# Retention fed in steps between MLA's blocks of queries; block 2's output projection in one pass

## The chip, the cores and the metric

The kernel runs on one core of one Trainium2 chip. The metric is the time of one execution on the device, in microseconds (us), as the median of several executions. The core has a matrix engine (PE, with its weight loads on a track of their own, PEld), a vector engine (DVE), a scalar engine (ACT), GpSimd (POOL), and SyncE (SP), which here only starts DMA transfers. Each engine carries out its own queue in order. PE's clock is granted at one of two levels, 1.2 and 2.4 GHz; the profile shows it as a share of full speed.

## What is computed

Two transformer blocks of two layers each over 512 tokens of 1024 features. The change lies in the second block. One of its layers, from the reference:

```python
hn = rms_norm_2(h, attn_norm[l])
proj = hn @ w_in[l]
p_a, p_b, p_c = ...                        # columns for RWKV-7, retention, MLA
y_a, v_first = rwkv7_mixer(p_a, ...)       # 256 features
y_b = retention_mixer(p_b, positions)      # 256 features, 4 heads, chunks of 128 tokens
y_c = mla_mixer(p_c, positions, ...)       # 512 features, 8 heads, causal softmax
mix = jnp.concatenate([y_a, y_b, y_c], axis=-1)
h = h + mix @ w_out[l]
hn = rms_norm_2(h, ffn_norm[l])
gu = hn @ w_gate_up[l]
h = h + (jax.nn.silu(gu[..., :D_FF_2]) * gu[..., D_FF_2:]) @ w_down[l]
```

Retention, per head and chunk: scores within the chunk times a decay mask times the values; the sum of the chunks before, decayed, as a 64x64 state that the decayed queries read; then a norm per head and a gate.

## The kernel before

Activations lie with features on the partitions: a tensor of 1024 features is eight tiles ("k-tiles") of 128 x 512. Every float32 product is made of three matmuls, high part by high part, low by high and high by low: `split` (L154, L155) makes the parts of an activation, `load_w` (L133 to L140) loads a weight tile by SP, casts it on ACT (`whi`) and subtracts on DVE (`wlo`). There are three buffers for each of `whi` and `wlo`, two for the raw weights, five for `tm`.

The program is written as a sequence, but a scheduler orders the instructions of each engine before the run: an instruction may go ahead of others that were written before it when its inputs are there. A pool of tiles that is opened where another was closed uses the same memory.

A layer of block 2 runs in these steps. RWKV is woven with the input projections of MLA and then of retention (`weave`, `ret_inputs`). `mla` (L1733) then goes over 8 heads, each in four blocks of 128 queries: scores (tags `l` and `m`, four matmuls), softmax on DVE and ACT, transposes (`t`), values (`o`); after each score block `feed` (L177) takes `rate` steps of the filler, which is the rest of `ret_inputs`, one step for two k-tiles of a projection. Two heads share the tile `yt`, which is one buffer (`y=(0,)`): `normalised` turns the softmax sums, sends them by DMA to memory and back as a broadcast, multiplies on POOL and writes the pair to `mixd` by DMA; the next pair's output is written into the same tile. After MLA, `retention` (L1682) runs for its two pairs of heads with banks `l`, `m`, `t`, `o`. Then eight tiles of the residual `X` are loaded again (L1890), in layer 0 also scaled (L1896, eight DVE instructions); the six tiles of RWKV and MLA are read back from `mixd` into `tm` (L1900) and split. `residual` makes the eight outputs from six k-tiles (weights `w2out`, adds at L869); a second pass over the eight outputs adds retention's two k-tiles (weights `w2outb`, adds at L1914) and calls `prepare` for each output: a square on ACT (L1097), its sum on POOL (L1098), and the split `hh`, `hl` for the feed-forward network (L1105, L1106), whose first matmuls read `hh` and `hl` of all eight outputs.

## Time and profile before

| | |
|---|---|
| median of 3 runs | 3397.08 us (3393.93 to 3398.56) |
| the profiled execution | 3398.97 us, of which its span is 3397.2 us |
| busy share of the span | PE 97%, PEld 81%, DVE 57%, ACT 36%, POOL 12% |
| mean granted clock of PE | 0.985 |
| layer 0 of block 2: MLA, retention, output projection | about 2148 to 2299 us of the span |
| layer 1 of block 2: the same | about 2871 to 3026 us |

A row of a timeline gives the start, the duration, the engine, the line, the operation, output and inputs, the shapes and the count, and in brackets the idle time of the engine just before and what ended it. A row of the stages gives the busy time of each engine in one stretch, with the number of instructions, the granted clock (1.00 is 2.4 GHz), the busy share of the DMA engines and their GB/s. Idle time of PE in a stretch is its length less PE's busy time.

### The profile page before, as it was taken

To read this page: it belongs to the slowest core of one execution; us is meant where nothing else is said; L and a number is where in the kernel's file an instruction comes from. 1 tells how busy PE (TensorE), PEld (TensorE's weight loads), DVE (VectorE), ACT (ScalarE), POOL (GpSimd) and SP (SyncE) were. 2 spreads that over 40 slices of the span, in tenths; PEclk is the share of its full clock that TensorE was granted. 3 is DMA by queue.
4 is the path that set the end of the run, shared out by engine and by line. 5 is a ranking of instruction groups with operands and counts; after the bars stand their busy time and mean duration, and the time that the engine had idled before them with its cause. 6 is when DMAs were issued, how large, how long until landed. Compare 5 with 4: busy or idle time off the path is not lost. (4 is left out here: it accounts for less than half of the span.)

```text
span 3397.2 us, 48949 instructions
## 1 busy us (share of the span) xinstructions
PE 3311.8 (97%) x19412; PEld 2747.3 (81%) x19412; DVE 1930.5 (57%) x3356; ACT 1233.3 (36%) x2196; POOL 398.5 (12%) x362
## 2 busy tenths in 40 slices
PE   7999999999999999999999999999999999999998
PEld 4888888888888888889888877777888777778887
DVE  6667765756444567757333466764434566754344
ACT  3566632311212346634222332532222332632222
POOL 4231000100000101101000301111101111121001
PEclk9999999999999999999999999999999998999999
DMA  6434373334334243253232323323233323422322
GB/s 215 132 114 125 109 264 109 112 118 132 123 128 129 73 137 106 91 187 111 93 90 98 125 80 98 118 89 93 89 98 99 109 69 97 128 89 94 94 98 81
DMA packets 138110, 385.86 MB, mean 114 GB/s; under 512 B 17492, under 2 KB 29268, under 8 KB 137880
## 3 DMA queue, kind: packets, MB, share of 16 engines
q1 hardware_dynamic: 134552, 372.15, 34.7%
q0 software_dynamic: 3328, 10.57, 1.0%
q8 instruction: 153, 2.51, 0.3%
q14 instruction: 77, 0.63, 0.1%
HBM read 331.56 MB, written 43.76 MB: 110 GB/s over the span
## 5 line engine op out<-in xcount | busy, mean ns | idle before, releaser
L139 ACT CAST whi<-raw 128x1024 fp32r<-128x1024 f32 (+4 forms) x436 | 435.4, 999 | 1288.5 <-PE b L158 870.7
L140 DVE TENSOR_TENSOR wlo<-raw,whi 128x1024 fp32r<-128x1024 f32 (+4 forms) x431 | 510.4, 1184 | 382.2 <-ACT whi L139 355.2
L158 PE MATMUL b<-hl,whi 128*128 128x512 f32 (+1 forms) x1760 | 688.2, 391 | 6.0 <-DVE hl L1106 5.5
L158 PE MATMUL b<-hh,whi 128*128 128x512 f32 (+1 forms) x1760 | 692.5, 393 | 0.0
L158 PE MATMUL b<-hh,wlo 128*128 128x512 f32 (+1 forms) x1760 | 686.9, 390 | 0.0
L158 PEld LDWEIGHTS b<-hl,whi 128*128 128x128 f32 x1760 | 333.6, 190 | 81.4 <-DVE hl L1106 8.3
L158 PEld LDWEIGHTS b<-hh,whi 128*128 128x128 f32 x1760 | 333.9, 190 | 78.4 <-issue 4.8
L158 PEld LDWEIGHTS b<-hh,wlo 128*128 128x128 f32 x1760 | 333.4, 189 | 75.5 <-issue 0.7
L158 PE MATMUL b<-ah,whi 128*128 128x512 f32 (+1 forms) x864 | 317.8, 368 | 0.0
L158 PE MATMUL b<-ah,wlo 128*128 128x512 f32 (+1 forms) x864 | 317.7, 368 | 0.0
L158 PE MATMUL b<-al,whi 128*128 128x512 f32 (+1 forms) x864 | 317.6, 368 | 0.0
L158 PEld LDWEIGHTS b<-ah,whi 128*128 128x128 f32 x864 | 162.3, 188 | 29.9
L158 PEld LDWEIGHTS b<-al,whi 128*128 128x128 f32 x864 | 162.3, 188 | 29.9
L158 PEld LDWEIGHTS b<-ah,wlo 128*128 128x128 f32 x864 | 162.3, 188 | 29.8
L947 DVE TENSOR_TENSOR tm<-tm,b 128x512 f32<-128x512 f32 (+1 forms) x112 | 70.0, 625 | 202.3 <-PE b L158 195.9
L408 DVE SCALAR_TENSOR_TENSOR wlo<-raw,silb 128x1024 f32<-128x1024 f32 x128 | 157.3, 1229 | 41.4 <-DMA raw<-in_ada1b 22.2
L158 PE MATMUL l<-hh,whi 128*128 128x512 f32 (+1 forms) x472 | 176.4, 374 | 0.8 <-DVE stB L697 0.3
L158 PE MATMUL l<-hl,whi 128*128 128x512 f32 (+1 forms) x472 | 173.2, 367 | 0.0
L158 PE MATMUL l<-hh,wlo 128*128 128x512 f32 (+1 forms) x472 | 172.7, 366 | 0.0
L508 DVE TENSOR_TENSOR pt<-t,pt 128x384 fp32r<-128x384 f32 (+2 forms) x272 | 131.1, 511 | 35.9 <-ACT pt L507 34.1
L158 PE MATMUL b<-hc,whi 128*128 128x256 f32 x800 | 141.5, 279 | 0.0
L467 DVE TENSOR_REDUCE st<-S 128x1 f32<-128x768 f32 (+2 forms) x160 | 121.7, 763 | 34.8 <-PE S L158 34.1
(572 smaller groups left out, 5784.0 us busy)
## 6 DMA issues: line engine op xcount, KB each, us to landing
raw<-in_wgu SPq DMA_DIRECT2D x92, 512.0 KB, 3.3
raw<-in_w2gu SPq DMA_DIRECT2D x88, 512.0 KB, 3.4
raw<-in_ada1b SPq DMA_DIRECT2D x48, 512.0 KB, 3.2
raw<-in_w2in SPq DMA_DIRECT2D x38, 512.0 KB, 3.5
raw<-in_ada0b SPq DMA_DIRECT2D x32, 512.0 KB, 4.2
raw<-in_wg SPq DMA_DIRECT2D x32, 512.0 KB, 3.9
raw<-in_w2d SPq DMA_DIRECT2D x32, 512.0 KB, 3.5
raw<-in_wd SPq DMA_DIRECT2D x24, 512.0 KB, 3.5
```

Source lines behind the costliest of these rows:

```text
L139: self.nc.scalar.copy(hi, raw)
L140: getattr(self.nc, self.lo).tensor_tensor(lo, raw, hi.bitcast(F32), op=ALU.subtract)
L158: self.nc.tensor.matmul(out, l, r, start=start, stop=stop)
L408: nc.vector.scalar_tensor_tensor(junk, raw, 0.5, self.silb[:, v], op0=ALU.mult, op1=ALU.mult, accum_out=m[:, w, k, v:v + 1])
L467: nc.vector.tensor_reduce(nm, S[:, lo:hi], axis=AX.X, op=ALU.max, negate=True)
L508: nc.vector.tensor_tensor(o, src, h.bitcast(F32), op=ALU.subtract)
L947: nc.vector.tensor_tensor(b, th, pu, op=ALU.mult)
```

## The change

Retention becomes a part of the filler. `retained` runs `ret_inputs` and then `retention`, which gives way at six places for each pair of heads, takes its banks from tag `b` (two banks), and writes its two k-tiles as number 2 and 3 into tiles that are set aside before MLA. `counted` counts the steps taken before MLA, and the rate in MLA is (52 less these) / 30 instead of 1. After MLA a pool of eight banks `b` is opened; the six other k-tiles are loaded and split, now ahead of the scaling of `X`. The output projection has one pass: the weights of the eight outputs are of eight k-tiles each and come in through `next_w`; outputs 0, 1 and 2 are opened with k-tiles 0 to 6, then each gets k-tile 7 (MLA's last pair of heads), then outputs 3 to 7 follow with eight k-tiles. `prepare` follows each output. The second pass and its weights are gone. The number of matmuls of the projection is the same (8 x 8 x 3 for a layer).

```diff
--- before.py
+++ after.py
@@ -33,6 +33,7 @@
+RSTEPS = 52
@@ -1239,10 +1240,17 @@
-    @staticmethod
-    def kept(gen, results):
-
-        results.append((yield from gen))
+    def counted(self, gen):
+
+        self.taken = 0
+        for x in gen:
+            self.taken += 1
+            yield x
+
+    def retained(self, l, pool, es, H, bc, rs, tab, mix):
+
+        src = yield from self.ret_inputs(l, [pool, pool], H, bc, rs, tab)
+        yield from self.retention(l, self.rets, src, mix)
@@ -1677,13 +1685,12 @@
-                + [d[f"w2v{l}"][c] for c in range(2)] + [w[11], w[12]])
+                + [d[f"w2v{l}"][c] for c in range(2)] + [w[11], w[12]] + [d[f"w2out{l}"][n] for n in range(KD)])
     def retention(self, l, pool, src, mix):
...
-            qd = self.t(pool, [128, 3, 128], F32, "rq", 2)
+            qd = self.t(pool, [128, 3, 128], F32, "rq", 1)
...
-            ps = self.bank("t")
+            ps = self.bank("b")
...
-            kt = self.t(pool, [128, 3, 128], F32, "rkt", 2)
+            kt = self.t(pool, [128, 3, 128], F32, "rkt", 1)
...
-            inner = [self.bank(next(tags)) for _ in range(2)]
+            yield
+            inner = [self.bank("b") for _ in range(2)]
...
+            yield
+            st = self.bank("b")[:, :192].rearrange("p (c e) -> p c e", e=64)
...
+            yield
+            pso = self.bank("b")
...
+            yield
+            bc = (yield from self.head_rstd_steps([sq], 1.0 / 64, EPS, "b", tok=(rt, rt2)))[0]
...
-            self.split(y, mix[0]["lat"][6 + p], mix[1]["lat"][6 + p])
+            self.split(y, mix[0]["lat"][2 + p], mix[1]["lat"][2 + p])
+            yield
@@ -1859,60 +1871,69 @@
-                    self.filler = self.streamed("L", self.kept(self.ret_inputs(l, [retp, retp], H, bc, rs, tab_r), results))
+                    self.filler = self.counted(self.streamed("L", self.retained(l, retp, es_rets, H, bc, rs, tab_r, mix)))
...
+            mp = self.pool(es_mix, "mixr")
+            for i in (2, 3):
+                mix[0]["lat"][i], mix[1]["lat"][i] = mixed(mp)
+            self.rets = self.pool(es_rets, "rets", "right")
             with ExitStack() as es:
                 self.stream = "A"
-                self.credit, self.rate = 0, 1.0
+                self.credit, self.rate = 0, (RSTEPS - self.taken) / 30
                 self.mla(l, self.pool(es, "mla"), slots, sm, mixd)
                 self.stream = "L"
             self.run(self.filler)
-            with ExitStack() as es:
-                self.retention(l, self.pool(es, "rets", "right"), ri, mix)
...
+            es_rets.close()
+            es_r.close()
+            es_ps.close()
+            es_l.close()
+            es_ps = ExitStack()
+            self.psum(es_ps, b=8)
             mp = self.pool(es_mix, "mix")
             for k_ in range(KD):
                 nc.sync.dma_start(out=X["lat"][k_], in_=self.xd[k_])
+            for i in (0, 1, 4, 5, 6, 7):
+                t = self.tm()
+                nc.sync.dma_start(out=t, in_=mixd[i])
+                mix[0]["lat"][i], mix[1]["lat"][i] = mixed(mp)
+                self.split(t, mix[0]["lat"][i], mix[1]["lat"][i])
             if l == 0:
...
-            order = [0, 1, 4, 5, 6, 7, 2, 3]
-            for i in range(6):
-                t = self.tm()
-                nc.sync.dma_start(out=t, in_=mixd[order[i]])
-                self.split(t, mix[0]["lat"][i], mix[1]["lat"][i])
-            self.residual(lambda n, k0, kn: d[f"w2out{l}"][n], 6, mix, X, 1, self.plan([LAT]), None)
-            es_ps.close()
-            es_l.close()
-            es_ps = ExitStack()
-            self.psum(es_ps, b=8)
...
-            for n in range(KD):
-                if n % 4 == 0:
-                    w = self.load_w(d[f"w2outb{l}"][n // 4])
-                ps, j = self.bank(), 2 * (n % 4)
-                self.proj([(w[0][:, j:j + 2], w[1][:, j:j + 2], (6, 7))], mix, LAT, ps)
-                nc.vector.tensor_tensor(X["lat"][n], X["lat"][n], ps, op=ALU.add)
-                done(LAT, n)
+            def products(n, ws, ps, kts):
+                for k_ in kts:
+                    hi, lo = (w[:, k_] for w in ws)
+                    xh, xl = (m["lat"][k_] for m in mix)
+                    self.mm(ps, hi, xh, k_ == 0, False)
+                    self.mm(ps, hi, xl, False, False)
+                    self.mm(ps, lo, xh, False, k_ == KD - 1)
+                if kts[-1] == KD - 1:
+                    nc.vector.tensor_tensor(X["lat"][n], X["lat"][n], ps, op=ALU.add)
+                    self.prepare(LAT, n, X, gcols("ffn_norm", l), H, [acc])
+
+            first = []
+            for n in range(W_BUFS):
+                first.append((n, self.next_w(), self.bank()))
+                products(*first[n], range(KD - 1))
+            for x in first:
+                products(*x, [KD - 1])
+            for n in range(W_BUFS, KD):
+                products(n, self.next_w(), self.bank(), range(KD))
@@ -2121,9 +2142,7 @@
-        out[f"w2out{l}"] = wtiles(np.concatenate([wo[:256], wo[512:]]))
-        out[f"w2outb{l}"] = np.ascontiguousarray(
-            wtiles(wo[256:512]).reshape(2, 4, 128, 2, 128).transpose(0, 2, 1, 3, 4)).reshape(2, 128, 8, 128)
+        out[f"w2out{l}"] = wtiles(wo)
```

## Rows read from the trace of the kernel before

**Rows 1.** Stages of both layers: length, busy us of each engine, clock, DMA.

```profile
2148.00:2195.00 47.00, 45.38 (x306) 38.16 (x305) 35.40 (x68) 35.45 (x95) 6.41 (x5) 1.00 0.44 128
2195.00:2212.00 17.00, 13.90 (x92) 11.74 (x91) 11.56 (x24) 10.90 (x30) 2.06 (x1) 0.90 0.49 160
2212.00:2226.00 14.00, 11.95 (x109) 9.68 (x109) 8.42 (x17) 6.83 (x16) 2.54 (x2) 1.00 0.47 152
2226.00:2244.00 18.00, 13.87 (x85) 9.87 (x81) 14.25 (x36) 4.43 (x8) 1.29 (x1) 0.81 0.12 44
...
2277.00:2291.00 14.00, 14.00 (x61) 10.91 (x59) 13.38 (x16) 8.90 (x14) 7.42 (x5) 1.00 0.24 75
2291.00:2299.00 8.00, 5.38 (x15) 3.35 (x15) 6.04 (x5) 3.56 (x6) 3.77 (x3) 0.79 0.18 66
2871.00:2925.00 54.00, 50.94 (x355) 43.33 (x354) 39.99 (x81) 35.68 (x95) 8.65 (x6) 1.00 0.39 116
2925.00:2940.00 15.00, 12.37 (x90) 10.26 (x88) 12.69 (x26) 12.01 (x33) 1.29 (x1) 1.00 0.66 208
2940.00:2953.00 13.00, 11.89 (x105) 9.60 (x106) 7.96 (x17) 6.59 (x17) 1.86 (x2) 1.00 0.55 163
...
3010.00:3026.00 16.00, 13.07 (x46) 9.39 (x45) 7.39 (x9) 5.45 (x8) 4.60 (x3) 0.79 0.21 67
```

**Rows 2.** Vector engine's instruction groups from 2277 to 2299: busy, mean ns, idle.

```profile
L1106 DVE SCALAR_TENSOR_TENSOR hl<-x,vec,hh 128x512 fp32r<-128x512 f32 x8 | 10.0, 1255 | 0.5 <-ACT hh L1105 0.5
L140 DVE TENSOR_TENSOR wlo<-raw,whi 128x1024 fp32r<-128x1024 f32 x4 | 5.6, 1400 | 2.1 <-ACT whi L139 2.1
L1914 DVE TENSOR_TENSOR x<-x,b 128x512 f32<-128x512 f32 x8 | 5.3, 678 | 0.1
```

**Rows 3.** PE in order of time, layer 0, where the feed-forward network begins.

```profile
2294.55 0.56 PE L158 MATMUL b<-hl,whi 128*128 128x512 f32 x1 [1.61 <-DVE hl L1106]
```

**Rows 4.** PE in order of time, layer 0, MLA's end and after.

```profile
2201.50 0.55 PE L162 MATMUL t<-cf,x 128*128 128x128 f32 x3 [2.93 <-ACT x L471]
...
2212.06 0.71 PE L158 MATMUL l<-qk,qk 96*128 96x512 f32 x2
...
2221.40 1.60 PE L158 MATMUL o<-mpt,mv 128*128 128x256 f32 x12 [0.67 <-DVE x L515]
2224.39 1.09 PE L158 MATMUL o<-rp,rv 128*64 128x128 f32 x16 [1.39 <-DVE x L515]
...
2226.22 0.49 PE L158 MATMUL b<-mh,whi 128*128 128x512 f32 x1
...
2237.15 0.80 PE L158 MATMUL b<-mh,whi 128*128 128x512 f32 x1 [3.98 <-DVE x L1896]
```

**Rows 5.** The line that scales the residual: ns least/median/most, first and last start.

```profile
L1896 DVE SCALAR_TENSOR_TENSOR x<-x,vec,b x8: 736/739/740, 2231.2 to 2236.4; 128x512 f32<-128x512 f32 x8
```

**Rows 6.** Stages at MLA's end, the matmuls on retention's queries and keys alone.

```profile
2212.00:2226.00 14.00, 5.11 (x35) 3.86 (x35) 0.00 (x0) 0.00 (x0) 1.00 0.47 152
2940.00:2953.00 13.00, 5.57 (x35) 4.16 (x35) 0.00 (x0) 0.00 (x0) 1.00 0.55 163
```

**Rows 7.** ACT in order of time, both layers, MLA's end.

```profile
2200.17 0.58 ACT L514 COPY x<-o 64x512 f32<-64x512 f32 x1 [2.63 <-DMA mix<-x]
...
2223.04 0.58 ACT L514 COPY x<-o 64x512 f32<-64x512 f32 x1 [2.05 <-PE o L158]
2223.64 1.66 ACT L154 CAST mh<-tm 128x512 fp32r<-128x512 f32 x3
...
2950.82 1.66 ACT L154 CAST mh<-tm 128x512 fp32r<-128x512 f32 x3
```

**Rows 8.** SyncE in order of time, layer 0: issues of the reads from mixd.

```profile
2198.91 1.89 SPq L1900 DMA_DIRECT2D tm<-mix  x4
```

**Rows 9.** PE in order of time, layer 1, one norm of retention.

```profile
2955.95 1.05 PE L158 MATMUL t<-cf,ry 128*128 128x2 f32 x8
...
2960.75 1.09 PE L158 MATMUL t<-cf,smlA 128*64 128x128 f32 x16
```

More of the change, by code (lines that the diff above doesn't have):

```diff
@@ L1685, in retention @@
         qk, vs, gs, rt, rt2 = src
-        tags = itertools.cycle("lm")
         hs = [slice(0, 64), slice(64, 128)]
@@ L1704, in retention @@
                     self.mm(v4(inner[h])[:, c], v4(k)[hs[h], c], v4(q)[hs[h], c], True, True)
-            st = self.bank("t")[:, :192].rearrange("p (c e) -> p c e", e=64)
-            for c in range(3):
-                for h in range(2):
-                    self.mm(st[hs[h], c], kt[:, c, hs[h]], val(c, h), True, True)
             w = []
@@ L1713, in retention @@
                 w.append(t)
+            yield
+            st = self.bank("b")[:, :192].rearrange("p (c e) -> p c e", e=64)
+            for c in range(3):
+                for h in range(2):
+                    self.mm(st[hs[h], c], kt[:, c, hs[h]], val(c, h), True, True)
             R = self.t(pool, [128, 3, 64], F32, "rst", 2)
@@ L1717, in retention @@
                 nc.vector.scalar_tensor_tensor(R[:, c], R[:, c - 1], tab[:, 8 + p, 0:1], st[:, c], op0=ALU.mult, op1=ALU.add)
-            pso = self.bank("o")
+            yield
+            pso = self.bank("b")
             for c in range(4):
@@ L1727, in retention @@
             nc.scalar.activation(sq, y, AF.Square)
-            bc = self.head_rstd([sq], 1.0 / 64, EPS, "t", tok=(rt, rt2))[0]
+            yield
+            bc = (yield from self.head_rstd_steps([sq], 1.0 / 64, EPS, "b", tok=(rt, rt2)))[0]
             nc.vector.scalar_tensor_tensor(y, y, 0.5, bc, op0=ALU.mult, op1=ALU.mult)
             nc.gpsimd.tensor_tensor(y, y, g, op=ALU.mult)
-            self.split(y, mix[0]["lat"][6 + p], mix[1]["lat"][6 + p])
+            self.split(y, mix[0]["lat"][2 + p], mix[1]["lat"][2 + p])
+            yield
     def mla(self, l, pool, slots, src, mix):
@@ L1861, in block2 @@
                 r, k, v, mis = self.rw_inputs(l, rp, H, bc, slots, ahead)
-                es_r, es_mix, es_ps = (ExitStack() for _ in range(3))
+                es_r, es_rets, es_mix, es_ps = (ExitStack() for _ in range(4))
                 retp = self.pool(es_r, "ret", "right")
+                mix = [{"lat": [None] * KD} for _ in range(2)]
                 with ExitStack() as er:
                     self.order_w(self.orders(l))
-                    results = []
-                    self.filler = self.streamed("L", self.kept(self.ret_inputs(l, [retp, retp], H, bc, rs, tab_r), results))
+                    self.filler = self.counted(self.streamed("L", self.retained(l, retp, es_rets, H, bc, rs, tab_r, mix)))
                     first = self.streamed("L", self.mla_inputs(l, self.pool(er, "fill", "right"), H, bc, rs, tab_m, sm, *self.acc2, self.filler))
@@ L1872, in block2 @@
             self.psum(es_ps, t=2, o=1, m=1)
+            mixed = lambda pool: [self.one(pool, [128, T], F32R, nm) for nm in ("mh", "ml")]
+            mp = self.pool(es_mix, "mixr")
+            for i in (2, 3):
+                mix[0]["lat"][i], mix[1]["lat"][i] = mixed(mp)
+            self.rets = self.pool(es_rets, "rets", "right")
             with ExitStack() as es:
                 self.stream = "A"
-                self.credit, self.rate = 0, 1.0
+                self.credit, self.rate = 0, (RSTEPS - self.taken) / 30
                 self.mla(l, self.pool(es, "mla"), slots, sm, mixd)
                 self.stream = "L"
-            self.lo = "vector"
             self.run(self.filler)
-            ri = results[0]
-            mp = self.pool(es_mix, "mix")
-            mix = self.feat(mp, KD, ["lat"], F32R, "mh"), self.feat(mp, KD, ["lat"], F32R, "ml")
-            self.lo = "vector"
-            self.stream = "A"
-            with ExitStack() as es:
-                self.retention(l, self.pool(es, "rets", "right"), ri, mix)
-            self.stream = "L"
-            es_r.close()
+            es_rets.close()
[4 more added lines that the diff above has]
+            self.psum(es_ps, b=8)
+            mp = self.pool(es_mix, "mix")
             for k_ in range(KD):
                 nc.sync.dma_start(out=X["lat"][k_], in_=self.xd[k_])
+            for i in (0, 1, 4, 5, 6, 7):
[3 more added lines that the diff above has]
+                self.split(t, mix[0]["lat"][i], mix[1]["lat"][i])
             if l == 0:
@@ L1896, in block2 @@
                     nc.vector.scalar_tensor_tensor(x, x, vec[:, V["final"] + k_:V["final"] + k_ + 1], b1, op0=ALU.mult, op1=ALU.mult)
-            order = [0, 1, 4, 5, 6, 7, 2, 3]
-            for i in range(6):
-                t = self.tm()
-                nc.sync.dma_start(out=t, in_=mixd[order[i]])
-                self.split(t, mix[0]["lat"][i], mix[1]["lat"][i])
-            self.residual(lambda n, k0, kn: d[f"w2out{l}"][n], 6, mix, X, 1, self.plan([LAT]), None)
-            es_ps.close()
-            es_l.close()
-            es_ps = ExitStack()
-            self.psum(es_ps, b=8)
-            acc = [self.acc, None]
-            done = lambda s, n: self.prepare(s, n, X, gcols("ffn_norm", l), H, [acc])
-            for n in range(KD):
-                if n % 4 == 0:
-                    w = self.load_w(d[f"w2outb{l}"][n // 4])
-                ps, j = self.bank(), 2 * (n % 4)
-                self.proj([(w[0][:, j:j + 2], w[1][:, j:j + 2], (6, 7))], mix, LAT, ps)
-                nc.vector.tensor_tensor(X["lat"][n], X["lat"][n], ps, op=ALU.add)
-                done(LAT, n)
+            acc = [self.acc, None]
+            def products(n, ws, ps, kts):
[16 more added lines that the diff above has]
+                products(n, self.next_w(), self.bank(), range(KD))
             es_mix.close()
```

## Prediction, made before the changed kernel was run

> **What bounds the kernel now.** The page comes first: PE is busy for 97% of the span and no other engine for more than 57%, so the time is PE's work, the times when PE waits, and the times when it runs at the lower clock. The change keeps every matmul (the projection has 8 x 8 x 3 for a layer either way, retention is only moved), so it can move the time only by the last two. The second view is therefore the table of stages [rows 1]: for each stage I take the idle time of PE (length less busy) and the loss by the clock (length times one less the mean clock; where PE is also idle this counts a little twice).
>
> In layer 0, MLA's body (2148 to 2195, 2195 to 2212) has 1.6 and 3.1 us idle, and 0.10 x 17 = 1.7 us by the clock. MLA's end (2212 to 2226) has 2.0 us idle. The start of the projection (2226 to 2244) has 4.1 us idle and 0.19 x 18 = 3.4 us by the clock. Its main part has next to nothing. Its junction with the feed-forward network (2291 to 2299) has 2.6 us idle and 0.21 x 8 = 1.7 us by the clock. In layer 1 the body has 3.1 and 2.6 us idle, the end 1.1, the start nothing that matters, the junction (3010 to 3026) 2.9 us idle and 0.21 x 16 = 3.4 us by the clock [rows 1]. That is some 33 us in all, 1.0% of the time; a step of this change is worth what it takes from it or puts to it.
>
> The third view is the timelines, for who ends those waits: at the junction `hl` of the vector engine [rows 3], at the start of layer 0's projection the scaling of the residual [rows 4], in MLA's body the softmax behind an ACT copy that waits for the DMA which frees the one `yt` [rows 4, 7].
>
> **The junction: minus 10.6 us.** In the second pass an output has 6 matmuls, at 14.00 us for 61 of them [rows 1] 0.23 us each or 1.4 us. The vector engine owes it an add (0.68), a split (1.26) and its share of weight subtractions (four of 1.40 for eight outputs, 0.70) [rows 2], 2.6 us, and it is busy for 13.4 of 14 us while PE still is for 14.0 [rows 1]. It falls behind, and the network's first matmuls wait for the last `hl`. With eight k-tiles an output takes 24 x 0.23 = 5.5 us of PE; the vector engine's 0.68 + 1.26 + 1.40 = 3.3 us fit. Behind output 7, PE has the seven other k-tiles of the network's first product, 21 matmuls or 4.8 us, and the chain for the eighth (add 0.7, a square and a cast on ACT at 0.55 each, as the three casts in [rows 7] take 1.66, and 1.3 for the split) is some 3.1 us. So both junctions go: 2.6 + 1.7 + 2.9 + 3.4 = 10.6 us. What is late next is nothing there; if a split is queued behind a weight subtraction, up to 1.4 us comes back for each layer, so the bounds are -10.6 and -8.
>
> **The start of layer 0's projection: minus 7.5 us.** PE stands still for 3.98 us until the scaling is over [rows 4]: eight instructions of 0.74 [rows 5], 5.9 us on the vector engine ahead of a split that PE needs. After it PE runs at the lower clock. In the new order the splits are written ahead of the scaling, and the three opened outputs give PE 3 x 21 x 0.23 = 14.5 us before it needs the last pair. That pair is ready late, not the others: in layer 0 the last copy of MLA starts at 2223.04 [rows 7], and the wait before the sixth k-tile ended at 2237.15, after the scaling; without the scaling it would be some 6 us earlier. 14.5 us cover either. I take the whole 4.1 + 3.4 = 7.5; should the scheduler still put the scaling first, only half goes: -7.5 to -3.5.
>
> **MLA's body: minus 4 us, from -9 to +8.** Counting the steps in the code: the gaps that RWKV yields add up to 75.0 and 76.0, which at 1.4 makes 53 and 54 steps; MLA's inputs take 42 of them and draw 4 more, so 15 and 16 steps of the filler are gone when MLA begins. Before, 23 and 22 of 38 are left for 32 feeds at rate 1, and the last nine feeds have no filler; those feeds are the stretches 2195 to 2212 and 2925 to 2940, with 4.8 and 2.6 us lost [rows 1]. After, the filler has 38 + 12 = 50 steps, the rate is 37/30 and 36/30, and it is used up at feed 29; retention's twelve steps lie on feeds 19 to 29, in just those stretches. They give PE something to do while ACT waits 2.63 us for `yt` [rows 7] and PE for it 2.93 us [rows 4]. But each step of retention needs the vector engine or ACT before the next, and in layer 1 those are busy for 12.7 and 12.0 of 15 us there [rows 1]. No row shows retention's chain inside MLA. The one nearest is a norm, where PE went from the sums to the spreading in 4.8 us, less its 1.05 of own work [rows 9]. From below, all of the 12.1 us of the body's losses but 3 go; from above, each of the four pairs costs half such a norm, 2 us, on top. I take a gain of 4 us, nearer to the first, because in `feed` MLA's work lies between the steps.
>
> **MLA's end: plus 12.2 us, from 0 to +21.** This is what the change pays. Between the last scores (2212.06) and the first matmul of the projection (2226.22) [rows 4] PE now works mostly on retention: 5.1 us on its queries and keys in layer 0, 5.6 in layer 1 [rows 6], and then 1.09 us on the values [rows 4]. After the change retention is used up before the last three feeds, and the softmax, transposes and values of the last head follow with nothing beside them. Can the opened outputs fill this? Their first matmul needs k-tile 0. The reads of four such tiles were issued from 2198.91 on [rows 8], but their casts start at 2223.64, directly behind MLA's last copy, though ACT had idled 2.05 us before that copy; the same in layer 1 at 2950.82 [rows 7]. So they wait for MLA's end, by its memory or by the order, and the change opens that pool at the same place. I take 5.1 + 5.6 = 10.7 us of new idle time, and 1.5 us by the clock for both layers. A stretch at the lower clock costs 1.7 to 3.4 us in [rows 1]; it came with an idle time of 3.98 us in one piece, not with 1.39 [rows 4], and here the pieces lie between. Bounds: nothing (the products fill it) to twice 7.2 us idle plus two stretches of 3.4.
>
> **Weights of output 3: plus 1.2 us, from 0 to 2.8.** Outputs 0 to 2 hold all three weight buffers until their k-tile 7. Output 3's cast and subtraction (1.40 [rows 2]) can only start behind output 0's last three matmuls, under the six of outputs 1 and 2 (1.4 us). I take 0.6 us a layer. Costed at nothing: the prefetch of the weights through `next_w` (same bytes, loaded while MLA runs as now), two weight loads fewer a layer, and eight adds fewer on a vector engine that has room there.
>
> **Sum.** -10.6 - 7.5 - 4 + 12.2 + 1.2 = -8.7 us. Against the profiled execution's 3398.97 this is 3390.3; the median of the runs lies 1.9 us below that execution, so I predict 3388 us. A measurement of this kernel can tell about 0.2%, 6.8 us, from no change.
>
> **Rivals.**
> (A) MLA's end is filled after all, by the opened outputs or because the scheduler lets retention slide there as now. For it: retention went ahead of its place before [rows 4, 6]. Against: the casts at 2223.64 [rows 7]. Without the 12.2 us the sum is -20.9: 3376 us.
> (B) The gains are given back. MLA's end costs 14.4 us idle and one clock stretch, 3.4, and the body gains nothing: -18.1 + 17.8 + 1.2 = +0.9, 3398 us. For it: the end is a chain by itself. Against: the feeds ahead of it are slower then, so the `yt` chain is over sooner.
> (C) Slower: retention's returns between PE and the vector engine hold up PE's queue, and the softmax behind it, inside MLA. The price is the norm's gap of 3.8 us [rows 9] and as much again for its four other returns, 8.5 us for a pair, 34 us for four; it decides once more than half of that, 17 us, is uncovered. Then -18.1 + 17 + 12.2 + 1.2 = +12.3, 3409 us. Against: ten feeds of MLA's own work lie between.
> (D) Retention's POOL instructions slow the vector engine in MLA. Splits that read two tiles of SBUF took 1.26 us beside busy POOL, an add with one input from PSUM 0.68 [rows 2]. If four POOL instructions a layer cost the vector engine 0.6 us each on the path, with B's end, the result is B's and a little more, about 3400 us. The Trainium skill ("SBUF — State Buffer", section "SBUF: two separate sides") speaks against the change here: it says that a vector instruction with two SBUF inputs and a GpSimd instruction that reads SBUF shut each other out for the whole instruction. The trace agrees with the 1.26 against 0.68 us.
>
> **How the numbers follow.** Forecast 0.47 (its own range 3382 to 3394), A 0.16, B 0.17, C 0.10, D 0.10. Faster by over 0.2% is below 3390.3: 0.40 of the forecast's 0.47 and A, 0.56. Slower: C, 0.10. The rest, 0.34, is within. The range from 3376 to 3400 takes in A, the forecast, B and D.
>
> **What would show it.** Right: no idle time by `hl` at the two junctions and clock 1.00 there; one pass with 24 matmuls in 5.5 us; no wait of PE behind the scaling; some 6 us more idle time of PE between the last scores and the first `mh`. Wrong: casts of `mh` ahead of MLA's last copy (A); waits of PE for `rkt`, `rp` or `rst` of over 1 us inside MLA, 17 us of them in all (C).

## The result: 37 us faster, 16.7 of them in code that the change does not touch

| | median, us | lowest to highest | runs |
|---|---|---|---|
| before | 3396.48 | 3393.93 to 3398.56 | 4 |
| after | 3359.07 | 3356.98 to 3367.33 | 4 |

The ratio is 0.9895, with a 95% interval from 0.9877 to 0.9913. The profiled execution of after took 3356.98 us with a span of 3355.1 us; PE is busy for 98% of it at a mean clock of 0.989. Predicted were 3388 us, from 3376 to 3400: the sign was right, the size was not, and the time lies below the range.

First the stages, as in [rows 1] (length, busy us of PE, PEld, DVE, ACT and POOL with their counts, clock, DMA share and GB/s).

```profile
2165.00:2180.00 15.00, 13.17 (x88) 10.94 (x86) 11.39 (x23) 10.15 (x26) 1.27 (x1) 1.00 0.56 178
2180.00:2195.00 15.00, 14.16 (x127) 11.23 (x128) 11.50 (x38) 10.93 (x31) 2.39 (x2) 1.00 0.37 106
2195.00:2205.00 10.00, 9.02 (x100) 7.30 (x96) 5.76 (x12) 4.82 (x13) 2.55 (x2) 1.00 0.28 91
2205.00:2215.30 10.30, 7.96 (x53) 6.20 (x53) 6.63 (x23) 4.72 (x11) 1.27 (x1) 0.83 0.44 129
2230.00:2261.00 31.00, 30.97 (x131) 24.33 (x130) 23.33 (x21) 15.28 (x21) 9.26 (x6) 1.00 0.38 119
...
2910.00:2922.60 12.60, 9.39 (x78) 7.50 (x74) 7.99 (x27) 7.62 (x19) 2.45 (x2) 0.99 0.43 131
2922.60:2932.00 9.40, 9.38 (x27) 7.06 (x28) 4.25 (x6) 2.25 (x5) 1.55 (x1) 0.65 0.35 107
...
2256.00:2272.00 16.00, 16.00 (x70) 12.84 (x69) 8.06 (x7) 4.92 (x7) 3.42 (x2) 1.00 0.33 98
2966.00:2982.00 16.00, 16.00 (x70) 12.88 (x69) 8.39 (x7) 5.24 (x7) 3.43 (x2) 1.00 0.31 99
```

The last two rows are the junctions with the feed-forward network: no idle time of PE and the full clock, where [rows 1] had 2.6 and 2.9 us idle at 0.79. The projection (2230 to 2261) has no gap. MLA's end still has some (2205 to 2215.3: 2.3 us), and in layer 1 the projection starts at the lower clock (0.65 over 9.4 us).

But that is only half of it. Block 1 is the same code in both kernels, and yet the first tile of the residual is written to memory at 1905.1 us of the span before and at 1889.2 us after. Nothing waits there less: from 500 to 1200 us PE is idle for 1.5 us before and 1.6 after. The groups of PE's instructions in that stretch (form, count, busy us, mean ns of one, idle) tell the two apart; before first, then after:

```profile
L158 PE MATMUL b<-hh,whi 128*128 128x512 f32 x400 | 158.0, 395 | 0.0
L158 PE MATMUL b<-hl,whi 128*128 128x512 f32 x400 | 157.8, 395 | 0.0
```

```profile
L159 PE MATMUL b<-hh,whi 128*128 128x512 f32 x400 | 156.0, 390 | 0.0
L159 PE MATMUL b<-hl,whi 128*128 128x512 f32 x400 | 155.9, 390 | 0.0
```

The same 512-column matmuls take 390 in place of 395 ns, and from the start of one to the start of the next (by the starts in the timeline) 226.7 in place of 233.3 ns, all along this stretch. Elsewhere in after the step from one to the next is 233.3 or 234.3, and the value switches at once where the matmuls go over to other tiles. So it does within block 1, from 1600 to 1900 us of after:

```profile
L159 PE MATMUL b<-hh,whi 128*128 128x512 f32 x295 | 116.5, 395 | 0.0
L159 PE MATMUL b<-ah,whi 128*128 128x512 f32 x138 | 53.7, 389 | 0.0
```

### The profile page after: what moved, and what is told of

Its sections match the earlier page's. It is cut to its first block, busy times and chain, and to the rows that moved or that the text cites. A ratio compares the mean times of both kernels' runs of the same rounds, so it can differ in the third digit from the quotient of the medians.

```text
span 3355.1 us, 48877 instructions
## 1 busy us (share of the span) xinstructions
PE 3281.4 (98%) x19412; PEld 2737.1 (82%) x19412; DVE 1923.1 (57%) x3336; ACT 1233.3 (37%) x2192; POOL 398.6 (12%) x362
## 3 DMA queue, kind: packets, MB, share of 16 engines
q1 hardware_dynamic: 133976, 372.15, 35.3%
## 5 line engine op out<-in xcount | busy, mean ns | idle before, releaser
L159 PEld LDWEIGHTS b<-hh,wlo 128*128 128x128 f32 x1760 | 330.8, 188 | 73.7 <-issue 0.7
L409 DVE SCALAR_TENSOR_TENSOR wlo<-raw,silb 128x1024 f32<-128x1024 f32 x128 | 157.6, 1232 | 45.3 <-DMA raw<-in_ada1b 24.5
```

Of the source, the lines that this page charges most:

```text
L159: self.nc.tensor.matmul(out, l, r, start=start, stop=stop)
L409: nc.vector.scalar_tensor_tensor(junk, raw, 0.5, self.silb[:, v], op0=ALU.mult, op1=ALU.mult, accum_out=m[:, w, k, v:v + 1])
```

## Experiments

Two kinds: why block 1 changed, and what each part of the change is worth in its own stretch. "Gain" is the time saved against the kernel before run on the same chip. For the second kind a stretch is measured in each trace, from MLA's first cast of values (`mv`) over the first and the last product of the projection to the 100th 512-column matmul of the feed-forward network. In the table each cell is layer 0 / layer 1, in us, and the last column is the sum of both layers.

| kernel | to the first product | first to last product | last product to the 100th | sum |
|---|---|---|---|---|
| before | 74.4 / 70.6 | 60.7 / 53.3 | 30.1 / 31.8 | 320.9 |
| b_low384 | 73.7 / 71.0 | 60.4 / 53.3 | 31.3 / 31.4 | 321.1 |
| after | 81.6 / 75.6 | 45.5 / 48.5 | 25.1 / 25.1 | 301.5 |
| b_one_pass | 98.1 / 91.4 | 45.2 / 46.3 | 25.1 / 25.1 | 331.2 |
| a_ret_behind | 96.9 / 91.6 | 46.4 / 47.0 | 25.1 / 25.1 | 332.1 |
| a_ret_early | 84.1 / 83.2 | 45.7 / 48.0 | 25.1 / 25.1 | 311.2 |
| a_ret_late | 90.3 / 80.3 | 45.9 / 47.6 | 25.1 / 25.1 | 314.3 |
| a_two_pass | 79.7 / 77.2 | 50.6 / 50.6 | 27.7 / 27.6 | 313.5 |
| a_not_opened | 81.0 / 76.9 | 49.5 / 50.2 | 25.1 / 25.1 | 307.7 |
| a_up384 | 80.6 / 75.7 | 45.3 / 45.8 | 25.1 / 25.1 | 297.6 |

A trace is of one execution. That of `a_not_opened` took 11 us more than the median of its runs, that of `a_ret_behind` 10, that of `a_up384` 6; and `a_up384`, which differs from after by the place of tiles alone, has a sum 3.9 us lower. So a difference of some 4 us between two sums says little.

### Block 1's tiles moved (b_low384, a_up384)

One thing of the change reaches block 1: the small tiles. Each stream of work has six small buffers in the pool of temporaries, and retention ran in MLA's stream "A", the only user of that stream's six tiles of 16 floats, 384 bytes per partition. In the changed kernel it runs in stream "L", the six are never made, the pool is 384 bytes shorter, and what lies above it starts 384 bytes lower: most of block 1's tiles. Those that are taken from the other end of memory stay where they were, among them the `hh` of block 1's second feed-forward network. `b_low384` does that alone to the kernel before:

```diff
-        return self.t(self.tmp, [128, 48 if self.stream == "L" else 16], F32, "sml" + self.stream, 6)[:, :n]
+        s = "R" if self.stream == "R" else "L"
+        return self.t(self.tmp, [128, 48 if s == "L" else 16], F32, "sml" + s, 6)[:, :n]
```

> The kernel before with one edit: the small tiles of MLA's stream (six of 64 bytes per partition, 384 bytes) are taken from the other stream's, so that every tile of block 1 lies 384 bytes lower, as it does in the changed kernel. Retention, the two passes and everything else stay. Theory P (place): block 1 is 16 us shorter after the change because the 512-column matmuls take another time at another start address; then this kernel is 15 to 19 us faster than the one before, about 3380 us, with the group of hh by whi from 500 to 1200 us at 390 ns in place of 395. Rival S (the order of instructions, or something else that comes with moving retention): this kernel takes the time of the one before within 3 us, and its matmuls stay at 395 ns.

Measured: 3379.48 us, ratio 0.9953 (0.9940 to 0.9966), a gain of 16.7 us, and 390 ns for the group. `a_up384` takes it back in the changed kernel:

```diff
+        nc.gpsimd.memset(self.one(self.tmp, [128, 96], F32, "pad"), 0.0)
```

> The changed kernel with one edit: a tile of 384 bytes per partition is put at the end of the pool of temporaries, so that block 1's tiles lie again where they lay before. P: 15 to 19 us slower than the changed kernel, about 3375 us, that is 20 to 25 us below the kernel before, which is what moving retention and the one pass are worth by themselves; matmuls of block 1 at 395 ns. S: 3359 us as the changed kernel, 390 ns.

Measured: 3372.98 us, ratio 0.9933 (0.9919 to 0.9946), a gain of 23.2 us, 14.2 us less than after; the group is back at 395 ns. So it is the place of the tiles (P), not the order of instructions (S), and the change without it is worth 20.7 to 23.2 us.

### What place means (mm_place)

```diff
     def all(self):
-        self.block1()
-        self.block2()
+        ...
+                self.mm(ps, a("wh", k), x("mh", k), k == 0, False)
+                self.mm(ps, a("wh", k), x("ml", k), False, False)
+                self.mm(ps, a("wl", k), x("mh", k), False, k == kt - 1)
+        ...
+        for w in (0, 32):
+            for m in range(16):
+                for _ in range(2):
+                    output("M" + L[m] + "W" + L[w // 8], 8 * m, w)
+        ...
```

> Leaves out the whole computation: after ten outputs to warm up, outputs of 24 matmuls of 512 columns as in the kernel, with the start address of the moving tiles stepped by 32 bytes over 512 (outputs MA to MP, with the weights at two places, WA and WE), then the start address of the weights stepped by 32 bytes (wA to wP, with the moving tiles at two places). P: the time from one matmul to the next differs by some 7 ns between places (226.7 and 233.3 ns in the two traces), in a pattern over the start address that repeats every 256 bytes if the places seen so far (64 and 224 slow, 192 fast, modulo 256) are the whole story; if the distance to the weights counts, the fast place moves along with them. S: one time at all places, within 1 ns.

The groups of matmuls by output (the second letter is the start of the moving tiles in steps of 32 bytes; WA is the first place of the weights, WE lies 128 bytes on; in the columns the mean ns of one stands ahead of the idle time):

```profile
L159 PE MATMUL MAWA<-mh,wh 128*128 128x512 f32 x16 | 6.2, 389 | 0.0
L159 PE MATMUL MBWA<-mh,wh 128*128 128x512 f32 x16 | 6.3, 395 | 0.0
L159 PE MATMUL MCWA<-mh,wh 128*128 128x512 f32 x16 | 6.2, 389 | 0.0
L159 PE MATMUL MEWA<-mh,wh 128*128 128x512 f32 x16 | 6.3, 395 | 0.0
L159 PE MATMUL MFWA<-mh,wh 128*128 128x512 f32 x16 | 6.3, 396 | 0.0
...
L159 PE MATMUL MAWE<-mh,wh 128*128 128x512 f32 x16 | 6.3, 395 | 0.0
L159 PE MATMUL MEWE<-mh,wh 128*128 128x512 f32 x16 | 6.2, 390 | 0.0
L159 PE MATMUL MGWE<-mh,wh 128*128 128x512 f32 x16 | 6.2, 389 | 0.0
```

With the weights 128 bytes on, the fast place of the moving tiles is 128 bytes on too (MA to ME, MC to MG). From start to start, by the distance of the moving tile from the weights modulo 256 bytes (weights at WA; 42 steps at each place, without the first two of each output):

| distance, bytes | 0 | 32 | 64 | 96 | 128 | 160 | 192 | 224 |
|---|---|---|---|---|---|---|---|---|
| ns | 226.7 | 233.4 | 228.9 | 233.6 | 233.5 | 234.1 | 233.5 | 233.1 |

From 256 to 480 bytes the row repeats. So does it (within 1.2 ns) when the weights are moved instead, by the opposite distance. The values are those of the full kernels, by the start addresses in the two programs: block 1's feed-forward tiles lie 128 bytes from the weights before (233.3) and 0 after (226.7), but for the `hh` of its second layer, 32 in both; block 2's `hh` 32 in both (233.3), its `ah` 32 before (233.3) and 160 after (234.3). The Trainium skill (TensorE: Matmul & The Clock Gate, section "Step-by-step: what each phase is for") says that the moving operand and the weight load have read ports of their own, so that loading the next weights takes no SBUF read bandwidth from the running matmul; a step that grows from 226.7 to 233.4 ns by the distance of the two start addresses alone does not fit that as it stands, and here the measurement decides. What in the memory makes the difference is not shown; nor is it shown that it is the weight load that the moving read meets, since every run loads the weights for each matmul.

### Both kernels at the fast place (a_aligned, b_aligned)

`a_aligned` adds two small tiles to the changed kernel:

```diff
+        nc.gpsimd.memset(self.one(self.pool(ctx, "low", "right"), [128, 8], F32, "low"), 0.0)
...
+        nc.gpsimd.memset(self.one(cp, [128, 24], F32, "up"), 0.0)
```

> The changed kernel with two small tiles added that are only written once (32 bytes at the top of the right-hand side of memory, 96 bytes ahead of block 2's tiles on the left), so that the moving tiles of the 512-column matmuls and of the context's 256-column ones start at a multiple of 256 bytes from the weights, which mm_place shows as the fast place. Counted by place, the changed kernel has 4248 matmuls at 32 bytes (+6.7 ns each), 1344 at 160 (+7.6) and 248 at others, 40 us in all; between the kernel before and b_low384 the same count gave 22 us where 16.7 were measured. P: 30 to 40 us faster than the changed kernel, 3319 to 3329 us, with hh by whi at 390 ns everywhere. If what counts is only block 1's stretch: 3359 us.

Measured: 3331.14 us, ratio 0.9829 (0.9812 to 0.9845), a gain of 63.4 us: 26.0 more than after, a little under the range. Three of PE's groups over the whole span, after first, then `a_aligned`:

```profile
L159 PE MATMUL b<-hh,whi 128*128 128x512 f32 x1648 | 654.9, 397 | 0.0
L159 PE MATMUL b<-ah,whi 128*128 128x512 f32 x656 | 257.8, 393 | 0.0
L159 PE MATMUL b<-hc,whi 128*128 128x256 f32 x800 | 141.5, 279 | 0.0
```

```profile
L160 PE MATMUL b<-hh,whi 128*128 128x512 f32 x1648 | 647.8, 393 | 0.0
L160 PE MATMUL b<-ah,whi 128*128 128x512 f32 x656 | 255.4, 389 | 0.0
L160 PE MATMUL b<-hc,whi 128*128 128x256 f32 x800 | 145.1, 283 | 0.0
```

The expectation was wrong for the context's 256-column matmuls: at distance 0 they take 283 ns, at 32 bytes 279. Their two weight groups lose 5.3 us of busy time (3.6 by `whi`, 1.7 by `wlo`). `b_aligned` does the same for the kernel before, with 128 bytes more in the temporaries:

```diff
+        nc.gpsimd.memset(self.one(self.pool(ctx, "low", "right"), [128, 8], F32, "low"), 0.0)
...
+        nc.gpsimd.memset(self.one(cp, [128, 24], F32, "up"), 0.0)
...
+        nc.gpsimd.memset(self.one(self.tmp, [128, 32], F32, "pad"), 0.0)
```

> The kernel before with three small tiles that are only written once (128 bytes in the temporaries, 32 at the top of the right-hand side, 96 ahead of block 2's tiles on the left), so that its matmuls' moving tiles start at a multiple of 256 bytes from the weights as in a_aligned; retention, the two passes and all else as before. Counted by place the kernel before loses 62 us (5592 matmuls at 32 bytes, 3592 at 128), this one 2 us; three quarters of the count were seen in the time so far (16.7 of 22, 28 of 40). P, with the place and the rest of the change adding up: about 47 us faster than before, 3349 us, and a_aligned's 3331 us is 18 to 21 us below it. If place pays less where PE waits for others more: 3355 to 3370 us.

Measured: 3348.59 us, ratio 0.9863 (0.9846 to 0.9879), a gain of 47.5 us where 47 were expected. With both kernels at the same places, the change is worth 63.4 - 47.5 = 15.9 us by the gains, 17.5 by the medians: under the 18 to 21 that were expected, but either gain is known to some 6 us only. `a_aligned` is the fastest kernel of this study.

### The one pass without retention in MLA (b_one_pass)

`b_low384` with the projection of the changed kernel; retention keeps its banks and its place behind MLA:

```diff
+            es_ps.close()
+            es_l.close()
+            es_ps = ExitStack()
+            self.psum(es_ps, b=8)
...
-            self.residual(lambda n, k0, kn: d[f"w2out{l}"][n], 6, mix, X, 1, self.plan([LAT]), None)
...
+            for n in range(W_BUFS):
+                first.append((n, self.next_w(), self.bank()))
+                products(*first[n], range(6))
+            for x in first:
+                products(*x, [6, 7])
```

> The kernel b_low384 (before, block 1's tiles 384 bytes lower) with the projection of the changed kernel and retention left where it was, behind MLA with its own banks: weights of eight k-tiles through next_w, outputs 0 to 2 opened with the six tiles of RWKV and MLA, then retention's two, casts ahead of the scaling. To be set against b_low384, 3379.5 us. By the prediction's terms the junction and the start go (-10.6 and -7.5) and output 3 waits for weights (+1.2): 17 us faster, 3362.5 us; moving retention into MLA would then be worth only the 3 us from there to the changed kernel's 3359.1. Rival: the old end of retention and the opening of the eight banks behind it stall PE as in a_ret_behind, and the one pass brings under 8 us by itself, 3372 us or more; then the gain hangs on retention in MLA.

Measured: 3389.98 us, ratio 0.9992 (0.9981 to 1.0003), a gain of 4.5 us, so 12 us slower than `b_low384`; the rival's direction, and further than it said. The stages, and PE's timeline, layer 0:

```profile
2202.00:2230.00 28.00, 16.92 (x131) 13.72 (x130) 12.78 (x42) 6.94 (x13) 3.50 (x3) 0.59 0.09 31
2230.00:2275.00 45.00, 45.00 (x192) 36.23 (x192) 29.66 (x30) 16.14 (x22) 10.07 (x7) 0.99 0.27 82
```

```profile
2213.15 1.98 PE L159 MATMUL t<-cf,smlL 128*64 128x128 f32 x16 [3.36 <-DVE smlL L1210]
...
2221.35 1.87 PE L159 MATMUL t<-cf,ry 128*128 128x2 f32 x8 [1.40 <-ACT ry L1728]
2226.19 1.97 PE L159 MATMUL t<-cf,smlL 128*64 128x128 f32 x16 [2.97 <-DVE smlL L1210]
2229.83 0.77 PE L159 MATMUL b<-mh,whi 128*128 128x512 f32 x1
```

The projection itself is as dense as in after (192 matmuls in 45 us). It does not wait for its inputs: the six tiles that open it were split by 2213.7. But its eight banks lie where retention's banks were, which by the code is why its first matmul comes behind retention's last, and for 28 us PE has retention alone: 11 us idle, clock 0.59. In the kernel before, the first pass of six k-tiles ran beside retention; the second pass was the price of that cover.

### Retention behind MLA, and earlier or later in it (a_ret_behind, a_ret_early, a_ret_late)

`a_ret_behind` holds retention's steps back in the changed kernel:

```diff
+        self.taken = 0
...
-            next(self.filler, None)
+            if self.taken < 38:
+                next(self.filler, None)
...
-                self.credit, self.rate = 0, (RSTEPS - self.taken) / 30
+                self.credit, self.rate = 0, 1.0
```

> The changed kernel with retention held back: in MLA the filler stops at its 38 steps of input projections, at rate 1 as before, and retention's twelve steps run behind MLA. The one pass, the opened outputs and the order of casts and scaling stay. By the terms of the prediction (body -4, end +12.2) retention in MLA costs 8 us, and this kernel would be some 8 us faster than the changed one, 3351 us. By rival A (the end filled, body -4) it would be 4 us slower, 3363 us; if the moved retention had filled all the stalls of the body, up to 12 us slower, 3371 us.

Measured: 3389.86 us, ratio 0.9983 (0.9974 to 0.9992), a gain of 6.3 us: 31 us slower than after, far beyond all three expectations. It is the state of `b_one_pass` reached from the other side, and takes the same time. Against after (gain 37.4 us) retention standing alone costs 31 us here and 33 us in `b_one_pass`, where with MLA's work between its steps it costs nothing that can be seen.

`a_ret_early`:

```diff
-RSTEPS = 52
+RSTEPS = 66
```

> The changed kernel with the rate of the filler in MLA at (66 less the steps taken) / 30, about 1.7 a feed in place of 1.2, so that retention is over some ten feeds before MLA's end and nothing of it is left to slide into the last blocks. The prediction's reasoning on MLA's end (an end with nothing beside it costs 10.7 us idle and 1.5 by the clock over both layers) says 5 to 12 us slower, 3364 to 3371 us. Rival, that the end of MLA is short whether or not retention lies there: within 3 us of 3359 us.

Measured: 3369.61 us, ratio 0.9938 (0.9925 to 0.9950), a gain of 24.9 us, 12.5 us less than after, at the upper end of what was expected. Layer 1's end, stages and timeline:

```profile
2900.00:2915.00 15.00, 13.38 (x123) 10.85 (x122) 9.78 (x27) 7.31 (x20) 2.51 (x2) 0.89 0.18 67
2925.00:2935.30 10.30, 5.48 (x29) 4.39 (x30) 4.33 (x9) 4.77 (x12) 0.86 (x1) 0.79 0.48 153
```

```profile
2931.17 2.82 PE L159 MATMUL o<-mpt,mv 128*128 128x256 f32 x12 [2.60 <-DVE x L516]
```

With nothing of retention left, the end of MLA is idle for 4.8 of 10.3 us, and the clock falls. But that is the smaller part of the loss: from the end of the last scores to the first product it takes 9.3 us in layer 0 and 10.6 in layer 1, only 0.4 and 3.1 more than after, while the body ahead of it takes 2.1 and 4.4 us more, with the clock at 0.89 for a stretch in each layer. `a_ret_late`:

```diff
-RSTEPS = 52
+RSTEPS = 46
```

> The changed kernel with the rate at (46 less the steps taken) / 30, about 1.0 a feed: one or two of retention's steps are left when MLA is over. a_ret_early has shown that an end of MLA without retention costs 10 us. If more of it at the end is better still, this kernel is 2 to 5 us faster than the changed one, 3354 to 3357 us; if what is left behind MLA stands alone and holds up the opening of the eight banks, as in a_ret_behind (31 us for all twelve steps), it is 3 to 8 us slower, 3362 to 3367 us.

Measured: 3370.91 us, ratio 0.9934 (0.9918 to 0.9949), a gain of 26.4 us, 11.0 less than after, more than was expected of either side. PE in layer 0, where retention's last step is left behind MLA:

```profile
2222.01 1.97 PE L159 MATMUL b<-cf,smlL 128*64 128x128 f32 x16 [5.67 <-DVE smlL L1210]
...
2225.64 0.77 PE L159 MATMUL b<-mh,whi 128*128 128x512 f32 x1
```

One norm behind MLA holds up the first product by 5.67 us idle. So the rate of 52 lies between two losses of 11 and 12.5 us.

### Two passes again, and no opened outputs (a_two_pass, a_not_opened)

`a_two_pass` puts the two passes back into the changed kernel:

```diff
+            order = [0, 1, 4, 5, 6, 7, 2, 3]
+            mix = [{"lat": [m["lat"][i] for i in order]} for m in mix]
+            self.residual(lambda n, k0, kn: d[f"w2out{l}"][n], 6, mix, X, 1, self.plan([LAT]), None)
...
+            for n in range(KD):
+                if n % 4 == 0:
+                    w = self.load_w(d[f"w2outb{l}"][n // 4])
+                ps, j = self.bank(), 2 * (n % 4)
+                self.proj([(w[0][:, j:j + 2], w[1][:, j:j + 2], (6, 7))], mix, LAT, ps)
...
```

> The changed kernel (retention in steps in MLA) with the two passes of the kernel before: six k-tiles with their adds, then retention's two, weights loaded by each pass, no outputs opened. This prices the one pass where retention is out of the way, which b_one_pass could not. By the prediction's junction term: 10.6 us slower than the changed kernel, 3370 us, with PE's waits for the last hl and the lower clock back at both junctions; with the wait for MLA's last pair in the first output (about 4.5 us a layer, by the last cast in the trace of the changed kernel) up to 20 us slower, 3379 us. Rival, that all of the gain hangs on where retention runs: within 3 us of 3359 us.

Measured: 3372.55 us, ratio 0.9939 (0.9925 to 0.9953), a gain of 24.7 us, 12.7 less than after. By the table, 2.5 us a layer come back behind the last product, and 5 and 2 between first and last, where PE waits for MLA's last pair. The total is near the 10.6 us that were expected, but not by what was expected: behind the last product only 5.1 us come back, and the clock there is 1.00, where `b_low384` has 0.89. The wait in layer 0:

```profile
2226.96 0.79 PE L159 MATMUL b<-mh,whi 128*128 128x512 f32 x1 [3.33 <-ACT mh L155]
```

`a_not_opened` makes each output in one go:

```diff
-            first = []
-            for n in range(W_BUFS):
-                first.append((n, self.next_w(), self.bank()))
-                products(*first[n], range(KD - 1))
-            for x in first:
-                products(*x, [KD - 1])
-            for n in range(W_BUFS, KD):
+            for n in range(KD):
```

> The changed kernel with each of the eight outputs made in one go, so that output 0 needs MLA's last pair after 21 matmuls. In the trace of the changed kernel the first product started at 2215.30 and the last ml was there at 2225.4, 21 matmuls take 4.9 us: PE would wait 4.5 to 5 us a layer. Theory: 9 to 13 us slower with the clock that such a wait costs, 3368 to 3372 us. Rival: the reading of the last pair moves up, or the three held weight buffers (the prediction's +1.2) pay it back: within 3 us of 3359 us.

Measured: 3366.19 us, ratio 0.9915 (0.9901 to 0.9929), a gain of 31.1 us, 6.3 less than after, where 9 to 13 were expected. The waits are 2.68 and 2.45 us, not 4.5 to 5. The cast that ends them is no earlier (done 9.1 and 9.7 us behind the first product, in after 9.3 and 9.8); PE works longer before it, with 26 matmuls and not 21 in layer 0, and with 21 in 7.3 us, some of them at the lower clock, in layer 1:

```profile
2232.89 0.50 PE L159 MATMUL b<-mh,whi 128*128 128x512 f32 x1 [2.68 <-ACT mh L155]
...
2951.42 0.49 PE L159 MATMUL b<-mh,whi 128*128 128x512 f32 x1 [2.45 <-ACT mh L155]
```

### The order of scaling and casts (a_scale_first)

```diff
-            for i in (0, 1, 4, 5, 6, 7):
-                t = self.tm()
-                ...
             if l == 0:
                 b1 = self.bank()
                 ...
+            for i in (0, 1, 4, 5, 6, 7):
+                t = self.tm()
+                ...
```

> The changed kernel with the scaling of the residual written ahead of the six casts, as before the change. The prediction's term for the start of layer 0's projection says 7.5 us slower, 3366.6 us, with PE waiting behind the scaling for its first ml; up to 14 us slower if the casts also wait for the reload of the residual, which landed 8 us after the first product. Rival: the scheduler puts the casts first wherever they are written: 3359 us.

Measured: 3359.21 us, ratio 0.9907 (0.9894 to 0.9920), a gain of 35.3 us: no difference from after that can be told. The vector engine, layer 0:

```profile
2217.38 4.19 DVE L156 TENSOR_TENSOR ml<-tm,mh 128x512 fp32r<-128x512 f32 x5
2225.10 5.36 DVE L1910 SCALAR_TENSOR_TENSOR x<-x,vec,b 128x512 f32<-128x512 f32 x8 [3.53 <-DMA x<-xd]
2230.38 0.68 DVE L156 TENSOR_TENSOR ml<-tm,mh 128x512 fp32r<-128x512 f32 x1
```

The scheduler put five splits ahead of the scaling however they were written, since the residual's reload lands late. The sixth, MLA's last pair, does come behind the scaling here, as it did before the change; PE does not wait for it, because the three opened outputs last until then.

## Why the prediction was right and wrong

**Missing: the place of the tiles, -16.7 us.** No term, no rival and not the range had it. The prediction started from "the change keeps every matmul, so it can move the time only by idle time and the clock". The step that failed is that sentence: the time of a matmul is not fixed by its shape (395 and 390 ns above). The diff showed it, had one asked what each edit does to the sizes of pools that are opened early: retention leaves stream "A", and a family of buffers goes. Without it the changed kernel would take some 3373 to 3376 us (by `a_up384` and `b_low384`), just under the range; the rest of the miss lies in the stretch that the change does touch.

**The junction: held, -12.5 for -10.6.** From the last product to the 100th matmul of the network it is 31.3 and 31.4 us in `b_low384`, 25.1 and 25.1 after. No wait for `hl` like [rows 3] is left, and a clock of 1.00 at both. Not all of it is the second pass: with two passes and retention in MLA (`a_two_pass`) the stretch takes 5.1 us more than after, not 12.5.

**The start of layer 0's projection: held, -7.0 for -7.5, for one of the two reasons given.** To the last product, layer 0's stretch went from 134.1 to 127.1 us, and layer 1's, which had no such wait, from 124.3 to 124.2. The order of writing was put first in the prediction; `a_scale_first` shows that it counts for nothing: five splits go ahead either way, and the opened outputs cover the sixth. The -7.0 is by subtraction, with nothing else in layer 0 taken to have changed; the idle time and the clock in this stretch of the trace (4.2 us and 0.94 in `b_low384`, 0.03 and 1.00 after) agree with it.

**MLA's body and end, and the weights of output 3: 0 in place of +9.4 (-4, +12.2, +1.2).** This is the step that was wrong within the stretch. By layer 1's 124.3 and 124.2 us and by what is left of layer 0, these three come to nothing. PE's idle time ahead of the first product is 6.7 and 6.4 us in `b_low384`, 7.4 and 5.8 after. The stages show which of the three was mis-sized. Body and end of layer 0, then of layer 1, cut where the last scores end; `b_low384`, then after:

```profile
2132.40:2192.80 60.40, 55.78 (x370) 47.10 (x370) 44.72 (x87) 45.25 (x122) 8.43 (x6) 0.97 0.42 128
2192.80:2206.10 13.30, 11.24 (x105) 9.16 (x105) 8.17 (x17) 6.16 (x15) 2.56 (x2) 1.00 0.51 158
2858.80:2917.30 58.50, 53.21 (x353) 43.95 (x352) 45.75 (x89) 45.47 (x125) 8.21 (x6) 1.00 0.44 135
2917.30:2929.80 12.50, 11.40 (x104) 9.28 (x104) 7.45 (x17) 5.70 (x14) 2.54 (x2) 1.00 0.55 167
```

```profile
2133.70:2206.40 72.70, 67.63 (x522) 56.40 (x522) 54.44 (x119) 51.20 (x131) 11.50 (x9) 1.00 0.43 128
2206.40:2215.30 8.90, 6.56 (x44) 5.10 (x42) 5.62 (x18) 3.81 (x10) 1.27 (x1) 0.81 0.41 120
2847.00:2915.20 68.20, 65.61 (x509) 54.98 (x508) 54.33 (x124) 50.02 (x132) 11.25 (x9) 1.00 0.45 138
2915.20:2922.60 7.40, 4.19 (x36) 3.11 (x36) 5.24 (x15) 4.46 (x11) 1.26 (x1) 0.98 0.39 123
```

In the prediction's measure (idle time plus the loss by the clock) the body's losses fall from 11.7 to 7.7 us, -4.0 as forecast; those of the end rise from 3.2 to 7.4, +4.2 in place of +12.2. So the mis-sized term is MLA's end. The end, layer 0, in PE's timeline:

```profile
2204.16 1.05 PE L159 MATMUL b<-cf,ry 128*128 128x2 f32 x8
...
2205.38 0.93 PE L159 MATMUL l<-qk,qk 96*128 96x512 f32 x3
...
2208.77 1.05 PE L163 MATMUL t<-cf,x 128*128 128x128 f32 x4 [0.92 <-ACT x L472]
...
2209.96 1.98 PE L159 MATMUL b<-cf,smlL 128*64 128x128 f32 x16
...
2215.30 0.97 PE L159 MATMUL b<-mh,whi 128*128 128x512 f32 x3 [1.15 <-ACT mh L155]
```

Two things were taken wrongly. The 5.1 and 5.6 us of retention's matmuls at the end [rows 6] were turned into idle time of the same length; but the end became shorter instead, from the end of the last scores to the first product 9.0 us after, where it was 13.5 before [rows 4], and its idle time rose by 0.3 and 2.1 us only, with the casts of `mh` still directly behind MLA's last copy, as predicted. And retention was not used up three feeds before the end: a norm's way over the vector engine made its last step slide past the last scores (2209.96, above). The price that was put on an end with nothing beside it is not settled by `a_ret_early`, though it loses 12.5 us: its ends have 1.5 and 3.9 us more idle time than those of `b_low384`, at a clock of 0.68 and 0.79, which makes 10.5 us in the prediction's measure; but against after most of its loss lies in the body. The weights of output 3 cost nothing: PE has 0.03 us idle in layer 0's projection. One loss was seen that no term named: layer 1's projection starts at the lower clock, 3.0 us longer than layer 0's; in `a_up384` it does not (45.8 us). What made up for these 3.0 us in layer 1's unchanged 124.2 is not shown.

**The rivals.** A had the sum of this stretch, -20.9, against 20.7 measured from `b_low384` to after; of its two mechanisms it was retention sliding into the end, not casts ahead of MLA's last copy. That its sum fits so well is in part luck: it took the end at nothing and the junction at -10.6, and they came to +4.2 and -12.5. B's end (14.4 us idle and a clock stretch) was not seen: even `a_ret_early` has 8.5 us idle there. C did not come: PE waited 0.98 us once for `rp` in layer 0 and 0.81 in layer 1, and retention's returns lie under MLA's work. But alone they cost 31 to 33 us. That this is near the 34 that C counted is luck, since much of it is the lower clock, which C left out (in `b_one_pass`, from the last scores to the first product, 11.7 and 11.2 us idle at a clock of 0.69 and 0.75). What kept C away is only that MLA's work lies between, as the prediction argued. D was not tested by itself; nothing that was measured calls for it. What it rests on is in the trace of before: in layer 0 a split `hl` takes 0.74 us while POOL is idle and up to 1.78 beside it.

Put together: -8.7, -16.7 for the place, -9.4 for the body, the end and the weights, -1.9 for the junction, +0.5 for the start make -36.2 us, where -37.4 were measured.

## What to carry to other kernels

Before an edit is costed at nothing, look at what it does to the sizes of pools, and compare the mean time of one matmul in stretches that the edit does not touch: a step there by one or two per cent, where PE waits for nothing, may come from start addresses and not from the schedule (here 395 against 390 ns); padding that moves the tiles back tells. A second pass, an extra add or an early bank can be the cover of a chain that nobody else hides; take it away only after that chain has been moved to where other work lies between its steps, and tune how late it ends, for too early and too late cost the same here. When work is taken out from beside a chain on an engine that runs in order, ask whether the chain waited for it: then it may grow shorter, and not idle, as MLA's end did here.

## What the runs showed of the hardware

The step (from the start of one matmul to the start of the next) of a stream of 512-column matmuls on the parts of split float32 tensors, each with its weight load, depends on the distance of the moving tile's start from that of the weights modulo 256 bytes: 226.7 ns at 0, 228.9 at 64, 232 to 234.3 elsewhere, up to 3.4%. Over some 9,700 such matmuls this was worth 47.5 us to the kernel before (`b_aligned`), 1.4% of its time, for three tiles that are written once. For the context's 256-column matmuls 0 is not the best place: each takes 283 ns there against 279 at 32 bytes.
